# Scattered expert sums read back two jobs earlier and added in four jobs, in a fused decoder block

## Chip, core and metric

One NeuronCore of a Trainium2 chip runs the whole program; the other cores are idle. The metric is the device time of one execution in microseconds (us). PE is TensorE's matmuls, DVE is VectorE, ACT is ScalarE, POOL is GpSimd, SP is SyncE, which here only issues DMAs.

## What is computed

A decoder block on 512 tokens of 1024 features: one input projection, a sparse attention over the 128 keys that an indexer picks (DSA), a sliding-window attention with sinks (SWA), a gated merge, an output projection, a first layer norm, and a mixture of experts with a second layer norm. What the change touches is the mixture:

```python
combine = (jax.nn.one_hot(expert_id, N_EXPERTS) * top_w[..., None]).sum(1)   # two experts a token
for e in range(N_EXPERTS):                                                   # 32 experts
    h = jax.nn.silu(xt @ w_gate[e]) * (xt @ w_up[e])
    out = out + combine[:, e:e + 1] * (h @ w_down[e])
x = layer_norm(ALPHA * x + ffn, ln2_g, ln2_b)
```

## The kernel before

The kernel is one straight program written in a tile framework. A planner of that framework sets each engine's order by its own estimate of time, except for instructions that are pinned to the program's order; it also chooses which buffer of a pool a new tile gets, and puts in the waits. The attention stages fill about the first 330 us, the merge, the output projection, the first norm and the routing go to about 420 us, and the experts follow.

**Pages.** Nearly all large data live in one pool of PAGES (22) buffers of 1 MiB, 128 partitions by 2048 floats (`page`, L158 before the change). A page of weights, of accumulators, of gathered rows, of values read back: all come from there, and a DMA that loads a new page waits until the page's earlier use is over. Smaller tiles of 512 floats come from `temp`: four buffers with the tag "ms", five with the tag "pt".

**Experts.** Each expert is given 64 slots. The work is a list of 17 jobs, numbered here from 0 by their place in the loop at the end (`for n, w in enumerate(work)`): jobs 0 to 7 and 9 to 16 take two experts each, job 8 is one tile for tokens beyond an expert's 64 slots (the overflow job). A job of two experts needs six pages of weights, in this order: the first half of gate and up for both experts, the second half for both (the second pair), and down for both. `stage`, called three jobs ahead, issues them on SP's queue by `load_pieces` (L751, L754).

**A job.** PE multiplies the gathered rows with gate and up in 32 products of 0.22 us (`up_part`), ACT and DVE make the hidden values h (`hidden`, L1124 and L1126), PE turns the next job's rows and h, then multiplies h with the down weights (`down_half`). Then the sums leave in one of two ways:

- Jobs 0 to 7 (SCATTER): the scaled sums go by an indirect DMA of POOL to a DRAM tensor `yp`, which has two places a token (`scattered`).
- Jobs 8 to 16: `down_proj` splits the scaled sums into a high and a low half (yh, yl; yy for the overflow job), each in a tile of 512 floats, `places` makes a matrix of token places (ct), and `combine` adds them: PE multiplies place and halves into a bank named qt, and DVE adds the bank to the accumulator `acc` (L1227). These products are run in the next job, behind its gate and up products; in job 16, between them.

**Read back.** What lies in `yp` is read back after all scatters, two pages for blocks 0 and 1, two for blocks 2 and 3 (`back_load`, L1204, at the end of jobs 10 and 11), and DVE adds them to `acc` one job later (`back_add`, L1212, jobs 11 and 12, four adds of 128x1024 each).

**The end.** The second norm's weights g2 (named ln2, gain and offset of 0.5 MiB each, L1332 and L1333) are issued between the last job's up and down pages. In job 16 DVE and ACT centre the first block with the gain as soon as its sums are complete (`centre`, L110 by a helper), before the last hidden product; `rest` finishes the four blocks and the rows of the last job.

Of the kernel before, what the change touches and what calls it, by code (L numbers as in the profile page):

```python
# [20 lines left out]
P = 128  # L21
# [10 lines left out]
RMS_EPS = 1e-6  # L32
PAGES = 22
WARM = 14
# [14 lines left out]
DUMMY = 1  # L49
G2_AT = 4  # L50
BR_AT = (5, 7)
# [23 lines left out]
K_EARLY = 1  # L75
BACK_AT = 10
LAST_N = (0, 1, 1, 2, 1, 2, 1, 0)
# [53 lines left out]
def block_kernel(ctx: ExitStack, tc: tile.TileContext, xT, x, w_tm, w_in, w_uv, w_br, w_out, relb, oh,  # L131
# [31 lines left out]

    def temp(dt, name, tag="ms"):
        return pages.tile([P, 512], dt, name=name, tag=tag, bufs={"ms": 4, "pt": 5}[tag])

# [369 lines left out]
    def swa_out(b, Ls):  # L536
        n = P if b == 0 else 2 * P
        py = pv_bank()
        parts = [(s, g) for s in range(n // P) for g in range(2)]
        pts = {}  # L540

        def turn(s, g):
            tp = tr_bank()
            for i in range(4):
                nc.tensor.transpose(tp[:, i * P:(i + 1) * P], Ls[g * 4 + i][:, s * P:(s + 1) * P], ident)
            pt = temp(F32, "ptb", "pt")
            if g == 0:
                nc.scalar.activation(pt, tp, AF.Copy)
            else:
                nc.vector.tensor_copy(pt, tp)  # L550
            pts[s, g] = pt

        turn(*parts[0])
        for x in range(len(parts)):
            if x + 1 < len(parts):
                turn(*parts[x + 1])
            fill(SWA_FILL[1])
            s, g = parts[x]
            nc.tensor.matmul(py[g * 64:(g + 1) * 64], vb[:, b + 1 - n // P + s, g * 64:(g + 1) * 64], pts[s, g],  # L559
                             start=(s == 0), stop=(s == n // P - 1))  # L560
        pv = py.rearrange("p (i t) -> p i t", i=4)
        ts = slice(b * P, (b + 1) * P)
        nc.scalar.activation(ybh[:, :, ts], pv, AF.Copy)
        nc.vector.tensor_sub(ybl[:, :, ts], pv, ybh[:, :, ts].bitcast(F32))
# [11 lines left out]

    post["q"] = post_q
    lg = {0: swa_logits(0)}
    swa_probs(0, *lg[0])
# [50 lines left out]
    def dsa_out(h, Ls):  # L630
# [4 lines left out]
        def turn(g):  # L635
            tp = tr_bank()
            w = 0
            for s in g:
                for b in range(s, NB):
                    nc.tensor.transpose(tp[:, w:w + P], Ls[b][:, s * P:(s + 1) * P], ident)  # L640
                    w += P
            ph, pl = temp(F32R, "ptah", "pt"), temp(F32R, "ptal", "pt")
            nc.scalar.activation(ph[:, :w], tp[:, :w], AF.Copy)
            nc.vector.tensor_sub(pl[:, :w], tp[:, :w], ph[:, :w].bitcast(F32))
            pts[g] = (ph, pl)
# [54 lines left out]

    need("q0")
    lg = {0: dsa_logits(0)}
    for h in range(8):
# [457 lines left out]
    def down_proj(hT, dn, w_):  # L1161

        r = []
        if len(dn) == 2:
            for hf in range(2):
                py = down_half(hT, dn, hf)
                yh_, yl_ = temp(F32R, "yh", "pt"), temp(F32R, "yl", "pt")
                nc.scalar.activation(yh_, py, AF.Copy, scale=w_)
                nc.vector.scalar_tensor_tensor(yl_, py, w_, yh_.bitcast(F32), op0=ALU.mult, op1=ALU.subtract)
                r.append((yh_, yl_))  # L1170
            return r
# [6 lines left out]
        for s in range(2):  # L1178
            yy = temp(F32R, "yy", "pt")
            a, b = (slice(z * 64, (z + 1) * 64) for z in (s, 1 - s))  # L1180
# [26 lines left out]

    def back_add(q, r):
        for b in range(2):
            for t in r:  # L1210
                a = acc[2 * q + b]
                nc.vector.tensor_add(a, a, t[:, b * D:(b + 1) * D])  # L1212

    def places(tk_):
        ct = temp(F32R, "ct", "pt")
        nc.vector.tensor_scalar(ct, iot, tk_, None, op0=ALU.is_equal)
        return ct
# [104 lines left out]
    work.insert(OV_AT, "ov")  # L1322
    jobs = {}

    def stage(w):
        if w == "ov":
            jobs[w] = overflow_tile(0.0)
        else:
            pg = functools.partial(gather, idx[:, w:w + 1]) if w else None
            if w == 15:  # L1330
                load_pieces(6 * w + G2_AT)
                nc.sync.dma_start(g2[:, 0:D], bcast(ln2_g, D))  # L1332
                nc.sync.dma_start(g2[:, D:2 * D], bcast(ln2_b, D))  # L1333
            load_pieces(6 * w + 6)
            es = (w, w + 16)
# [103 lines left out]

    early, back, done_early = {}, {}, False  # L1440
    for n, w in enumerate(work):
        if n % 2 == 0 and 4 + n < 16:
            slots(4 + n, 6 + n)
        if n == 2:
            overflow_tiles()
        if n + 4 == len(work):
            g2 = page(F32, "ln2")
        if n + 3 < len(work):
            stage(work[n + 3])
        _, up, dn, tk_, w_ = jobs.pop(w)  # L1450
        last = n + 1 == len(work)
# [34 lines left out]
        if not last:  # L1486
# [4 lines left out]
            if w in SCATTER:  # L1491
                scattered(w, hT, dn, w_)
                late = []
            else:
                y = down_proj(hT, dn, w_)
                late = combine(places(tk_), y, then if n + 2 == len(work) else None)
        for q in range(2):
            if n == BACK_AT + q:
                back[q] = back_load(q)
            if n == BACK_AT + q + 1:  # L1500
                back_add(q, back.pop(q))
    pick(pz, [1], [0])
# [108 lines left out]
```

## Time and profile before

| | us |
|---|---|
| median of three runs | 714.94 (714.76 to 715.67) |
| the profiled execution, its own time | 714.15 |
| its span, on which the times of the rows are counted from 0 | 712.3 |
| PE busy | 650.9 (91%) |
| DVE busy | 394.5 (55%) |
| ACT busy | 261.3 (37%) |

The page divides the span in 40 slices of 17.8 us. A digit is the busy share of an engine in a slice in tenths. Each page of 1 MiB is one DMA, cut over 16 DMA engines. The views used below are the page, the list of who waited for whom, the order of time of one engine or queue, the instructions of one tile, groups of instructions, and busy times in chosen stretches.

### The profile page before, as it was taken

To read this page: it belongs to the slowest core of one execution; us is meant where nothing else is said; L and a number is where in the kernel's file an instruction comes from. 1 tells how busy PE (TensorE), PEld (TensorE's weight loads), DVE (VectorE), ACT (ScalarE), POOL (GpSimd) and SP (SyncE) were. 2 spreads that over 40 slices of the span, in tenths; PEclk is the share of its full clock that TensorE was granted. 3 is DMA by queue.
4 is the path that set the end of the run, shared out by engine and by line. 5 is a ranking of instruction groups with operands and counts; after the bars stand their busy time and mean duration, and the time that the engine had idled before them with its cause. 6 is when DMAs were issued, how large, how long until landed. Compare 5 with 4: busy or idle time off the path is not lost.

```text
span 712.3 us, 9305 instructions
## 1 busy us (share of the span) xinstructions
PE 650.9 (91%) x3394; PEld 435.8 (61%) x3394; DVE 394.5 (55%) x968; ACT 261.3 (37%) x552; POOL 90.9 (13%) x93
## 2 busy tenths in 40 slices
PE   7999998999999999999999989999998990679990
PEld 4788886766788878778899963334343440334430
DVE  6685999867444443667627882422135340654484
ACT  5563422867355445744214232121131120112260
POOL 0010000000000000012201333222221110110083
PEclk9999999999999999999999999999999996799996
DMA  8972511011411111154957779999999999998002
GB/s 326 359 253 73 193 60 59 2 60 59 178 60 59 60 60 59 61 178 163 385 220 296 265 268 375 421 418 419 416 418 420 418 417 418 414 420 361 15 19 120
DMA packets 34748, 164.65 MB, mean 231 GB/s; under 512 B 5977, under 2 KB 11361, under 8 KB 18828
## 3 DMA queue, kind: packets, MB, share of 16 engines
q1 hardware_dynamic: 26636, 147.98, 52.6%
q0 software_dynamic: 5968, 12.90, 5.1%
q10 hardware_dynamic: 2096, 3.15, 1.3%
q8 instruction: 28, 0.46, 0.3%
q14 instruction: 20, 0.16, 0.1%
HBM read 156.62 MB, written 16.29 MB: 243 GB/s over the span
## 4 chain that ended last, share of the span: by engine, by line
PE 65%; DMA 16%; DVE 14%; issue 2%; ACT 1%; POOL 1%; POOLq 0%; SPq 0%; DVEq 0%; ACTq 0%
PE mm L177 10%; PE mm L179 9%; PE mm L178 9%; DMA wexp<-in_w_up_dram 9%; PE mm L1076 8%; PE pv L1076 5%; PE qt L1076 4%; DMA wexp<-in_w_dn_dram 3%; DMA back<-yp 3%; DVE pgS L429 3%; DVE mx L427 2%; PE pv L559 2%; DVE whl L174 1%; PE tr L640 1%; DVE zb L110 1%
## 5 line engine op out<-in xcount | busy, mean ns | idle before, releaser
L177 PE MATMUL mm<-xh,whl 128*128 128x512 f32 (+1 forms) x272 | 108.4, 399 | 0.8 <-ACT xh L173 0.8
L178 PE MATMUL mm<-xl,whl 128*128 128x512 f32 (+1 forms) x272 | 106.3, 391 | 0.8 <-DVE xl L174 0.8
L179 PE MATMUL mm<-xh,whl 128*128 128x512 f32 (+1 forms) x272 | 106.2, 391 | 0.0
L1076 PE MATMUL mm<-wexp,xg 128*64 128x512 f32 x448 | 102.7, 595 | 1.8 <-DMA wexp<-in_w_up_dram 1.8
L1076 PEld LDWEIGHTS mm<-wexp,xg 128*64 128x64 f32 x448 | 31.7, 137 | 60.6 <-issue 55.6
L177 PEld LDWEIGHTS mm<-xh,whl 128*128 128x128 f32 x272 | 51.7, 190 | 12.7 <-issue 3.6
L179 PEld LDWEIGHTS mm<-xh,whl 128*128 128x128 f32 x272 | 51.5, 189 | 12.1 <-issue 2.5
L178 PEld LDWEIGHTS mm<-xl,whl 128*128 128x128 f32 x272 | 51.5, 189 | 10.0 <-DVE xl L174 1.1
L174 DVE TENSOR_TENSOR whl<-wraw,whl 128x1024 fp32r<-128x1024 f32 x34 | 41.5, 1221 | 25.7 <-ACT whl L173 24.0
L1076 PE MATMUL pv<-wexp,hT 128*64 128x512 f32 x240 | 55.3, 603 | 0.0
L796 POOL TENSOR_TENSOR tg<-tg 128x512 f32<-128x512 f32 x8 | 12.1, 1516 | 300.3 <-DVE tg L698 296.1
L1126 DVE TENSOR_TENSOR h<-h,mm 128x256 f32<-128x256 f32 x14 | 5.9, 420 | 66.0 <-ACT h L1124 66.0
L1076 PE MATMUL qt<-yh,ct 128*128 128x512 f32 x48 | 21.0, 437 | 22.8 <-DVE acc L1227 22.8
L173 ACT ACTIVATE whl<-wraw 128x1024 fp32r<-128x1024 f32 x34 | 35.7, 1054 | 14.1 <-DMA wraw<-in_w_in_dram 7.7
L1124 ACT ACTIVATE h<-mm 128x256 f32<-128x256 f32 x14 | 5.4, 384 | 94.4 <-PE mm L1076 94.4
L1227 DVE TENSOR_TENSOR acc<-acc,qt 128x512 f32<-128x512 f32 x56 | 34.3, 679 | 5.2 <-PE qt L1076 5.2
L1076 PEld LDWEIGHTS pv<-wexp,hT 128*64 128x64 f32 x240 | 16.8, 139 | 31.9 <-issue 27.4
L177 PE MATMUL mm<-woh,merged 128*128 128x256 f32 x120 | 36.3, 302 | 0.0
L1093 ACT ACTIVATE xg<-qt 128x512 f32<-128x512 f32 x32 | 18.0, 596 | 45.8 <-PE qt L1076 45.8
L178 PE MATMUL mm<-wol,merged 128*128 128x256 f32 x120 | 34.0, 283 | 0.0
L179 PE MATMUL mm<-woh,merged 128*128 128x256 f32 x120 | 33.9, 283 | 0.0
L1083 POOL MEMSET xg<- 128x1024 f32 x16 | 15.2, 953 | 137.0 <-PE qt L1076 137.0
(387 smaller groups left out, 1311.2 us busy)
## 6 DMA issues: line engine op xcount, KB each, us to landing
wexp<-in_w_up_dram SPq DMA_DIRECT2D x64, 1024.0 KB, 20.7
wexp<-in_w_dn_dram SPq DMA_DIRECT2D x31, 1024.0 KB, 20.8
wraw<-in_w_in_dram SPq DMA_DIRECT2D x16, 1024.0 KB, 4.9
yp<-routes SPq DMA_DIRECT2D x8, 512.0 KB, 8.5
braw<-in_w_br_dram SPq DMA_DIRECT2D x4, 1024.0 KB, 4.8
woraw<-in_w_out_dram SPq DMA_DIRECT2D x4, 1024.0 KB, 7.2
back<-yp SPq DMA_DIRECT2D x4, 1024.0 KB, 20.3
xraw<-in_xT_dram SPq DMA_DIRECT2D x4, 512.0 KB, 7.0
```

Source lines behind the costliest of these rows:

```text
L173: nc.scalar.activation(hi, raw, AF.Copy)
L174: nc.vector.tensor_sub(lo, raw, hi.bitcast(F32))
L177: nc.tensor.matmul(o, a[0], b[0], start=start, stop=False)
L178: nc.tensor.matmul(o, a[0], b[1], start=False, stop=False)
L179: nc.tensor.matmul(o, a[1], b[0], start=False, stop=stop)
L427: pin(nc.vector.max(out=mx, in_=acc))
L429: pin(nc.vector.match_replace(out=acc, in_to_replace=mx, in_values=acc, imm_value=GONE))
L559: nc.tensor.matmul(py[g * 64:(g + 1) * 64], vb[:, b + 1 - n // P + s, g * 64:(g + 1) * 64], pts[s, g], start=(s == 0), stop=(s == n // P - 1))
L1076: return lambda *a, **k: (pin if self.n else (lambda i: i))(getattr(nc.tensor, f)(*a, **k))
L1083: nc.gpsimd.memset(pg, 0.0)
L1093: nc.scalar.activation(c, banks[q], AF.Copy)
L1227: nc.vector.tensor_add(a, a, pc)
```

## The change

Five things are edited.

1. `BACK_AT` goes from 10 to 8: the back pages are issued at the end of jobs 8 and 9.
2. The adds are spread: in each of the jobs 11 to 14 one page, which is two adds of 128x1024.
3. PAGES goes from 22 to 23. The tag "pt" with its five tiles is gone; in its place a page of the pool holds four temporaries (`four_temps`, `temp4`), taken once for SWA, once for DSA, and once at job 8 for the halves of all following jobs. The tag "ms" has five buffers instead of four and now holds `ct` too.
4. The second norm's weights are issued after the last job's down pages.
5. The page for them is taken in `stage`, at the time of the load.

```diff
-PAGES = 22
+PAGES = 23
-G2_AT = 4
-BACK_AT = 10
+BACK_AT = 8
+BACK_ADD = 11
...
-    def temp(dt, name, tag="ms"):
-        return pages.tile([P, 512], dt, name=name, tag=tag, bufs={"ms": 4, "pt": 5}[tag])
+    def temp(dt, name):
+        return pages.tile([P, 512], dt, name=name, tag="ms", bufs=5)
+    turns = {"n": 0}
+    def four_temps(dt):
+        turns["page"] = page(dt, "four")
+    def temp4():
+        i = turns["n"] % 4
+        turns["n"] += 1
+        return turns["page"][:, i * 512:(i + 1) * 512]
...
-            pt = temp(F32, "ptb", "pt")
+            pt = temp4()
...
-            ph, pl = temp(F32R, "ptah", "pt"), temp(F32R, "ptal", "pt")
+            ph, pl = temp4(), temp4()
...
-                yh_, yl_ = temp(F32R, "yh", "pt"), temp(F32R, "yl", "pt")
+                yh_, yl_ = temp4(), temp4()
...
-            yy = temp(F32R, "yy", "pt")
+            yy = temp4()
...
-    def back_add(q, r):
+    def back_add(q, t):
         for b in range(2):
-            for t in r:
-                a = acc[2 * q + b]
-                nc.vector.tensor_add(a, a, t[:, b * D:(b + 1) * D])
+            a = acc[2 * q + b]
+            nc.vector.tensor_add(a, a, t[:, b * D:(b + 1) * D])
     def places(tk_):
-        ct = temp(F32R, "ct", "pt")
+        ct = temp(F32R, "ct")
...
+            load_pieces(6 * w + 6)
             if w == 15:
-                load_pieces(6 * w + G2_AT)
-                nc.sync.dma_start(g2[:, 0:D], bcast(ln2_g, D))
-                nc.sync.dma_start(g2[:, D:2 * D], bcast(ln2_b, D))
-            load_pieces(6 * w + 6)
+                norm2.append(page(F32, "ln2"))
+                nc.sync.dma_start(norm2[0][:, 0:D], bcast(ln2_g, D))
+                nc.sync.dma_start(norm2[0][:, D:2 * D], bcast(ln2_b, D))
...
+                if combined == 0:
+                    four_temps(F32R)
+                combined += 1
                 y = down_proj(hT, dn, w_)
...
-        for q in range(2):
-            if n == BACK_AT + q:
-                back[q] = back_load(q)
-            if n == BACK_AT + q + 1:
-                back_add(q, back.pop(q))
+        if 0 <= n - BACK_AT < 2:
+            back[n - BACK_AT] = back_load(n - BACK_AT)
+        if 0 <= n - BACK_ADD < 4:
+            back_add((n - BACK_ADD) // 2, back[(n - BACK_ADD) // 2].pop(0))
```

SP's queue before, from the last down page of job 13 to the first page of job 15. A row is a DMA: line, what is written, what is read. `wexp` is a page of weights, `back` a page read back, `yp` the scattered sums:

```order
L754 DMA wexp_4865<-in_w_dn_dram 128x2048
L1204 DMA back_4960<-yp_114 128x2x1024
L1204 DMA back_4962<-yp_114 128x2x1024
L751 DMA wexp_4964<-in_w_up_dram 128x2048
L751 DMA wexp_4966<-in_w_up_dram 128x2048
L751 DMA wexp_4968<-in_w_up_dram 128x2048
L751 DMA wexp_4970<-in_w_up_dram 128x2048
L754 DMA wexp_4972<-in_w_dn_dram 128x2048
L754 DMA wexp_4974<-in_w_dn_dram 128x2048
L1204 DMA back_5073<-yp_114 128x2x1024
L1204 DMA back_5075<-yp_114 128x2x1024
L751 DMA wexp_5077<-in_w_up_dram 128x2048
```

and of the change, from the last down page of job 11 to the first page of job 13:

```order
L767 DMA wexp_4623<-in_w_dn_dram 128x2048
L1217 DMA back_4678<-yp_114 128x2x1024
L1217 DMA back_4680<-yp_114 128x2x1024
L764 DMA wexp_4682<-in_w_up_dram 128x2048
L764 DMA wexp_4684<-in_w_up_dram 128x2048
L764 DMA wexp_4686<-in_w_up_dram 128x2048
L764 DMA wexp_4688<-in_w_up_dram 128x2048
L767 DMA wexp_4690<-in_w_dn_dram 128x2048
L767 DMA wexp_4692<-in_w_dn_dram 128x2048
L1217 DMA back_4772<-yp_114 128x2x1024
L1217 DMA back_4774<-yp_114 128x2x1024
L764 DMA wexp_4798<-in_w_up_dram 128x2048
```

Each pair of back pages stands two jobs, twelve pages of weights, further forward in the queue; the weights of jobs 12 and 13 stand behind them.

DVE before, from the halves of job 10 to the additions of job 12 (`yl` a low half, `ct` places, `h` hidden values, `acc<-acc,back` an add of a page read back, `acc<-acc,qt` one of PE's additions):

```order
L1169 SCALAR_TENSOR_TENSOR yl<-pv,wsl,yh 128x512 x2
L1216 TENSOR_SCALAR ct<-iot,tok 128x512
L1126 TENSOR_TENSOR h<-h,mm 128x256
L1212 TENSOR_TENSOR acc<-acc,back 128x1024 x4
L1227 TENSOR_TENSOR acc<-acc,qt 128x512 x8
L1169 SCALAR_TENSOR_TENSOR yl<-pv,wsl,yh 128x512 x2
L1216 TENSOR_SCALAR ct<-iot,tok 128x512
L1126 TENSOR_TENSOR h<-h,mm 128x256
L1227 TENSOR_TENSOR acc<-acc,qt 128x512 x4
L1212 TENSOR_TENSOR acc<-acc,back 128x1024 x4
L1227 TENSOR_TENSOR acc<-acc,qt 128x512 x4
```

and of the change, from the hidden values of job 11 to the second add of job 12:

```order
L1139 TENSOR_TENSOR h<-h,mm 128x256
L1239 TENSOR_TENSOR acc<-acc,qt 128x512 x8
L1228 TENSOR_SCALAR ct<-iot,tok 128x512
L1224 TENSOR_TENSOR acc<-acc,back 128x1024 x2
L1182 SCALAR_TENSOR_TENSOR four<-pv,wsl,four 128x512 x2
L1139 TENSOR_TENSOR h<-h,mm 128x256
L1239 TENSOR_TENSOR acc<-acc,qt 128x512 x8
L1228 TENSOR_SCALAR ct<-iot,tok 128x512
L1224 TENSOR_TENSOR acc<-acc,back 128x1024 x2
```

The adds came in two lots of four, ahead of or among PE's additions; they now come in four lots of two, behind a job's places and ahead of its own halves.

DVE before, around the halves of the overflow job (`yy`; `G` is a table that finds a job's slots):

```order
L1132 TENSOR_TENSOR h<-h,mm 64x256
L1182 SCALAR_TENSOR_TENSOR yy<-pv,ovs,yy 64x512
L1216 TENSOR_SCALAR ct<-iot,ovs 128x512
L1182 SCALAR_TENSOR_TENSOR yy<-pv,ovs,yy 64x512
L1227 TENSOR_TENSOR acc<-acc,qt 128x512
L1126 TENSOR_TENSOR h<-h,mm 128x256
L1227 TENSOR_TENSOR acc<-acc,qt 128x512 x7
L971 TENSOR_TENSOR G<-iot,routes 128x512 x2
```

and of the change:

```order
L1145 TENSOR_TENSOR h<-h,mm 64x256
L1228 TENSOR_SCALAR ct<-iot,ovs 128x512
L1139 TENSOR_TENSOR h<-h,mm 128x256
L1228 TENSOR_SCALAR ct<-iot,tok 128x512
L984 TENSOR_TENSOR G<-iot,routes 128x512 x2
L1195 SCALAR_TENSOR_TENSOR four<-pv,ovs,four 64x512 x2
L1239 TENSOR_TENSOR acc<-acc,qt 128x512 x8
```

The overflow job's two halves now stand behind the hidden values, the places and the slot tables of the next job.

## Rows read from the trace of the kernel before

**Rows 1.** The page's part 2: forty slices of the span.
```profile
PE   7999998999999999999999989999998990679990
...
PEclk9999999999999999999999999999999996799996
...
GB/s 326 359 253 73 193 60 59 2 60 59 178 60 59 60 60 59 61 178 163 385 220 296 265 268 375 421 418 419 416 418 420 418 417 418 414 420 361 15 19 120
```
**Rows 2.** Who waited for whom, PE, 440 to 712 us: us in total, times, longest.
```profile
PE qt L1076 <- DVE acc L1227: 27.2, 2, 22.8
```
**Rows 3.** PE in order of time: start us, us, line, op, [idle before].
```profile
579.51 7.04 PE L1076 MATMUL mm<-wexp,xg 128*64 128x512 f32 x32
...
611.60 0.80 PE L1076 MATMUL qt<-yh,ct 128*128 128x512 f32 x1 [22.79 <-DVE acc L1227]
...
619.38 7.04 PE L1076 MATMUL mm<-wexp,xg 128*64 128x512 f32 x32
...
634.90 1.83 PE L1076 MATMUL qt<-ident,xg 128*128 128x128 f32 x8 [4.38 <-DVE acc L1227]
...
641.04 7.03 PE L1076 MATMUL mm<-wexp,xg 128*64 128x512 f32 x32
...
672.33 1.89 PE L110 MATMUL mm<-wexp,xg 128*64 128x512 f32 x8
...
679.03 1.08 PE L110 MATMUL mm<-wexp,xg 128*64 128x512 f32 x4
```
**Rows 4.** DVE in order of time.
```profile
606.06 2.36 DVE L1212 TENSOR_TENSOR acc<-acc,back 128x1024 f32<-128x1024 f32 x2 [18.61 <-DMA back<-yp]
...
629.63 4.62 DVE L1212 TENSOR_TENSOR acc<-acc,back 128x1024 f32<-128x1024 f32 x4
...
685.55 2.12 DVE L110 SCALAR_TENSOR_TENSOR zb<-acc,mv,ln 128x768 f32<-128x768 f32 x1
```
**Rows 5.** Stretches: us, busy (x) of PE, PEld, DVE, ACT, POOL, granted clock, DMA.
```profile
611.00:614.60 3.60, 3.00 (x7) 2.42 (x8) 3.56 (x7) 0.00 (x0) 0.00 (x0) 0.50 1.02 422
635.00:638.50 3.50, 3.50 (x14) 1.92 (x16) 1.64 (x3) 1.20 (x2) 1.44 (x2) 0.51 1.00 417
```
**Rows 6.** SP's queue in order of time, jobs 12 to 16 and back pages.
```profile
553.96 7.80 SPq L751 DMA_DIRECT2D wexp<-in_w_up_dram  x4
...
569.73 7.85 SPq L751 DMA_DIRECT2D wexp<-in_w_up_dram  x4
...
586.03 2.85 SPq L1204 DMA_DIRECT2D back<-yp  x2
590.99 7.81 SPq L751 DMA_DIRECT2D wexp<-in_w_up_dram  x4
...
611.05 9.33 SPq L751 DMA_DIRECT2D wexp<-in_w_up_dram  x4
...
626.76 7.85 SPq L751 DMA_DIRECT2D wexp<-in_w_up_dram  x4
```
**Rows 7.** The tile wexp, 560 to 662 us: issues (ns), and us to landing.
```profile
L751 SPq DMA_DIRECT2D wexp<-in_w_up_dram x17: 327/328/572, 561.4 to 634.3; - x17
...
DMA to landing us min/median/max: 17.9/20.9/22.0
```
**Rows 8.** The tile back, whole span.
```profile
DMA to landing us min/median/max: 19.9/20.3/20.7
```
**Rows 9.** Who waited for whom, SP's queue, 400 to 660 us.
```profile
SPq L751 <- PE pv L1076: 25.0, 5, 16.3
```
**Rows 10.** Groups of DVE, 530 to 560 us: busy us, mean ns, idle before.
```profile
L1182 DVE SCALAR_TENSOR_TENSOR yy<-pv,ovs,yy 64x512 fp32r<-64x512 f32 x2 | 1.5, 749 | 5.7 <-ACT yy L1181 5.7
...
L971 DVE TENSOR_TENSOR G<-iot,routes 128x512 bf16<-128x512 f32 x2 | 1.3, 682 | 0.0
```
**Rows 11.** Stretches of the attention stage, columns as in rows 5.
```profile
110.00:140.00 30.00, 26.88 (x131) 20.05 (x130) 27.91 (x88) 17.18 (x55) 0.00 (x0) 1.00 0.10 36
140.00:200.00 60.00, 60.00 (x275) 41.28 (x275) 36.71 (x100) 35.33 (x87) 0.00 (x0) 1.00 0.24 88
```

More of the change, by code (lines that the diff above doesn't have):

```diff
@@ L577, in block_kernel @@
     post["q"] = post_q
+    four_temps(F32)
     lg = {0: swa_logits(0)}
@@ L1322, in block_kernel @@
     work.insert(OV_AT, "ov")
-    jobs = {}
+    jobs, norm2 = {}, []
     def stage(w):
@@ L1438, in rest @@
                                      in_=zs[:, 0:D], in_offset=None, bounds_check=T - 1, oob_is_err=False)
-    early, back, done_early = {}, {}, False
+    early, back, done_early, combined = {}, {}, False, 0
     for n, w in enumerate(work):
@@ L1445, in block_kernel @@
             overflow_tiles()
-        if n + 4 == len(work):
-            g2 = page(F32, "ln2")
         if n + 3 < len(work):
             stage(work[n + 3])
+        if n + 4 == len(work):
+            g2 = norm2[0]
         _, up, dn, tk_, w_ = jobs.pop(w)
@@ L1494, in block_kernel @@
             else:
+                if combined == 0:
+                    four_temps(F32R)
+                combined += 1
                 y = down_proj(hT, dn, w_)
                 late = combine(places(tk_), y, then if n + 2 == len(work) else None)
-        for q in range(2):
-            if n == BACK_AT + q:
-                back[q] = back_load(q)
-            if n == BACK_AT + q + 1:
-                back_add(q, back.pop(q))
+        if 0 <= n - BACK_AT < 2:
+            back[n - BACK_AT] = back_load(n - BACK_AT)
+        if 0 <= n - BACK_ADD < 4:
+            back_add((n - BACK_ADD) // 2, back[(n - BACK_ADD) // 2].pop(0))
     pick(pz, [1], [0])
```

## The prediction

> **What bounds the kernel now.** I read the page's busy lines first, then the waits of PE, then the order of time on PE, DVE and SP's queue. The first view shows that the second half of the span is not like the first: from the 26th slice to the 36th the DMA engines move about 418 GB/s without a break, and PE, at 9 tenths or more nearly everywhere, falls to 0 and 6 tenths in two slices, where its granted clock falls too [rows 1]. So two resources must be watched together: the stream of expert weights, and PE, which eats it.
>
> The list of waits names what stops PE there: 27.2 us in two waits, both on DVE's add into acc [rows 2]. In order of time, PE's first products of jobs 12, 13, 14 and 16 begin at 579.51, 619.38, 641.04 and 672.33 [rows 3]. Jobs 14 and 15 are undisturbed and take 31.29 us, 15.65 each; the steps 12 to 13 and 13 to 14 take 39.87 and 21.66. The excess is 24.2 + 6.0 = **30.2 us**. DVE's rows say why: its eight adds of the pages read back stand in two lumps, the first waits 18.61 us for its page to land, and the adds of PE's results into acc, which free the banks that PE wants, queue behind [rows 4]. The excess is more than the 27.2 us of waits because PE comes back from each at a granted clock of 0.5, the lower of its two levels (1.2 GHz) [rows 5].
>
> **What this buys at most.** SP's queue issues the pages of weights in order, one every 2.5 us, and a page lands about 20.9 us (back pages and those beside them 20.3) after its issue [rows 6 to 8]. Adding that to the issue of the fourth page of a job (the end of its row, less the 0.33 us of one issue) gives when its up projection has all it needs: job 12 at 582.3, job 13 at 598.2, job 14 at 618.8, job 15 at 640.4, job 16 at 655.2. PE wants the second pair 3.5 us after a job begins (half of a row of 7.04 us [rows 3]), so job 12 wants it at 583.0 and has it 0.7 us before. PE and the stream were level when the stall came. The stall let the stream run ahead, and without it PE must wait for weights. Not all of the 30.2 us can be had.
>
> **The change, part by part.**
>
> *Read back earlier.* The four back pages go two jobs forward in SP's queue, before the weights of jobs 12 and 13. One pair takes 590.99 - 586.03 = 4.96 us of the queue [rows 6]. So the weights of job 12 come 5.0 us later than now, those of job 13 9.9, those of job 14 5.0, those of jobs 15 and 16 as now. The stream moves the same bytes. Walk PE through it, with 8.6 us from the end of one job's products to the start of the next (15.65 less 7.04):
>
> - job 12 starts at 579.5, wants its second pair at 583.0, has it at 587.3, ends its products at 590.8;
> - job 13 starts at 599.4, wants it at 602.9, has it at 608.1, ends at 611.6;
> - job 14 starts at 620.2, wants it at 623.7, has it at 623.8, ends at 627.3;
> - job 15 starts at 635.9, wants it at 639.4, has it at 640.4, ends at 643.9;
> - job 16 starts at 652.5; its products stand among the previous job's additions, so the second pair is wanted 6.7 us after the start (672.33 to 679.03 [rows 3]), at 659.2, and is there at 655.2.
>
> Job 16 started at 672.33; the gain is **19.8 us**. About 10 of the 30 us come back as waits for weights.
>
> The Trainium skill, on its page "DMA: Bandwidth & Descriptors", section "Where 436 GB/s comes from", says that between HBM and SBUF the HBM side binds at some 358 GB/s. By that figure a page would take 2.93 us, the two pairs 11.7 instead of 9.9, and the gain would be 1.8 us less. The trace disagrees: 418 GB/s over eleven slices [rows 1], so the sum keeps 2.5 us a page.
>
> *Two blocks in each of jobs 11 to 14.* The eight adds, 2.36 us a pair [rows 4], are the same work; now two stand behind the job's places and ahead of its halves on DVE. The first back page takes the place in the queue that the first weight of job 12 has now, an issue at 553.96, so it lands at about 574.9 and its two adds are done at 577.3; the halves behind them come from PE's down products of job 11, which are the last thing before job 12's start at 579.5. Cost 0: what little a half is late lies under the 7 us of job 12's up products, and only after these does PE want it. Without that cover, 2.4 us a job on DVE, 9.4 in all.
>
> *A page for four temporaries.* The pool has one page more, and the four temporaries take it from job 8 on, and in the two attention stages. Until job 8 the weights have one page more to run ahead, and before that SP had waited up to 16.3 us at a time for PE to free a page [rows 9]. A page is worth 2.5 us of the stream, if it is issued into time that DMA has free; at worst nothing. I take 1.5, nearer the upper end because the wait for a page is long. Carried through the walk above (every landing 1.5 us earlier), job 16 starts at 651.0: a gain of **21.3 us**.
>
> *The order of the overflow job's halves.* On DVE they now stand behind the next job's hidden product, its places and two slot tables: two tables 1.3 us and two halves 1.5 [rows 10]. PE's additions of the overflow job wait for them: 0 to 2.8 us, at job 9. I take 2.8, but it costs nothing at the end: PE then comes to job 12 at 582.3, wants the second pair at 585.8, and that lands at 585.8; job 13 waits for its weights in any case.
>
> *The attention stage.* Four slots replace five, and the scheduler sets some of PE's products there in another order. From 140 us on PE is full in it (60.00 of 60 us), and the 30 us before lack 3.1 [rows 11]; the same products remain, so a new order gains at most those 3.1 and loses, by the same row, as much again: -3 to +3 us. I take 0; the 1.5 us above has room for it.
>
> *Second norm's weights last.* The last two pages of weights come 2.5 us earlier, where nothing waits for them. The norm's own land behind them, at 655.2 + 4 x 2.5 - 1.5, some 663 at the latest for both halves and 1.3 earlier for the half that DVE wants first. DVE wants it at 685.55 now [rows 4], so at 664.2 after. Hidden, with 1 to 2.5 us of cover. If it is late, job 16's hidden product stands behind that row on DVE, and PE's last products behind the hidden product: microsecond for microsecond.
>
> **Sum.** The profiled execution took 714.15 us, the median of the runs is 714.94, 0.8 above. 714.94 - 21.3 = **693.6**; I say 693.5.
>
> **The rivals.**
>
> *Less waiting for weights* (0.13). If the stream gains the whole page and the pairs wait less, the bound is the last page: job 16's second pair at 655.2 - 2.5, so a start at 646.0 and a gain of 26.3: 688.6. For: 30.2 us are there. Against: SP's steady 2.5 us.
>
> *The clock* (0.17). Today a wait of 4.38 us is followed by a stretch of 3.5 us at clock 0.51 [rows 3, 5]. The new waits at jobs 12 and 13 are of that size (4.3 and 5.2), and may each bring such a stretch, in which 1.75 us are lost, part of it under the wait for the second pair. One to two stretches: 695 to 697. The Trainium skill, "TensorE: Matmul & The Clock Gate", section "HAM oscillation — how this bites in real kernels", tells of a kernel that waited for DMA at every piece of work and came back slow every time; by that rule each new wait pays, and the time is the upper end of this rival. The trace agrees for both waits on acc: each is followed by the slow clock [rows 5].
>
> *The norm's weights or the attention order cost what I called hidden* (0.15): 2 to 4 us, 695.5 to 698.
>
> *Starved of pages: slower* (0.03). The back pages are now held for three to five jobs. With 23 pages, 2 of acc, 2 of gathered rows, 1 of temporaries and 4 read back leave 14; a running job holds 6; 8 are in flight (20.9 over 2.5). That is just enough. If the pool's assignment makes a job's first weight wait for the job directly before it, a job takes 20.9 + 7.0 = 27.9 us instead of 15.65, in jobs 11 to 14 +49; less the 30.2 removed, 734. It decides from two pages more held than I count. Against: from 400 to 660 us SP waited for PE only five times, 25.0 us in all, 16.3 of them at once [rows 9].
>
> *It doesn't do what it says* (0.02): the reads still land late for the adds. SP's new order speaks against it.
>
> **How the numbers follow.** The forecast (691 to 695) has 0.50. Below 688.5 and above 699 I leave some 2 in 10: the range is 688.5 to 699.0, from the first rival's bound to no page gained with two slow stretches. A measurement of this kernel tells 0.2% (1.4 us) from no change. Faster 0.95, the same 0.02, slower 0.03.
>
> **What would show it.** Right: PE has no wait on acc's add left; instead one on weights at jobs 12 and 13, 3 to 6 us each; DVE's adds of back pages stand in four pairs with no idle time before them; DMA stays near 418 GB/s till some 660; job 16's first product at about 651. Wrong: SP waiting for PE between 550 and 640, DVE waiting for the norm's weights, or a job 16 that starts before 646 or after 656.

## The result, and the profile after

The changed kernel takes **697.32 us** (median of four runs, 697.11 to 699.07), against 715.31 us for the kernel before. The ratio is 0.9746, with a 95% interval of 0.9714 to 0.9777: faster by 2.5%. The forecast was 693.5 us in a range of 688.5 to 699.0. The sign and the mechanism came out; the time is 3.8 us longer than forecast, and the experiments are mostly about those 3.8 us. The profiled execution took 697.48 us, its span is 695.7, so the span is 16.6 us shorter than before.

The page's part 2 of the changed kernel answers to [rows 1]:

```profile
PE   7899998999999999999999987999999799899990
...
PEclk9999999999999999999999999899999899989995
...
GB/s 315 377 247 82 212 62 60 1 61 61 182 60 62 61 60 8 83 154 125 338 326 195 317 243 381 258 418 419 419 417 417 421 415 415 417 419 419 371 35 132
```

The hole of PE is gone: no slice but the last is under 7 tenths. The stream of weights keeps its 418 GB/s from the 27th slice on. The 26th slice (435 to 452 us) is new in another way: DMA moves only 258 GB/s there.

Who PE waited for, 330 to 712 us, largest first, answers to [rows 2]:

```profile
PE qt L1089 <- DMA xg<-x1d,idx: 4.7, 1, 4.7
PE mm L1089 <- DMA wexp<-in_w_up_dram: 3.1, 2, 1.7
PE qt L1089 <- DVE four L1195: 2.6, 2, 1.9
```

The 27.2 us of waits for DVE's add into acc are gone. The waits for weights that the forecast put in their place are there, but smaller and both at job 13 (3.1 us in all, not some 10 over jobs 12 and 13), and the largest wait is one that nobody forecast: for gathered rows (xg), before the first expert.

PE in order of time, the first products of jobs 0, 12, 13 (in two pieces), 14 and 16, and the waits, answers to [rows 3]:

```profile
433.52 1.97 PE L1089 MATMUL qt<-ident,xg 128*128 128x128 f32 x8 [4.75 <-DMA xg<-x1d,idx]
...
435.85 1.98 PE L1089 MATMUL mm<-wexp,xg 128*64 128x512 f32 x4
...
587.44 7.04 PE L1089 MATMUL mm<-wexp,xg 128*64 128x512 f32 x32
...
604.65 1.04 PE L1089 MATMUL mm<-wexp,xg 128*64 128x512 f32 x2 [1.37 <-DMA wexp<-in_w_up_dram]
607.38 10.01 PE L1089 MATMUL mm<-wexp,xg 128*64 128x512 f32 x30 [1.69 <-DMA wexp<-in_w_up_dram]
...
625.98 7.04 PE L1089 MATMUL mm<-wexp,xg 128*64 128x512 f32 x32
...
657.27 1.89 PE L110 MATMUL mm<-wexp,xg 128*64 128x512 f32 x8
```

Job 16 begins at 657.27, 15.1 us earlier than before; the forecast said 651.0. Job 12 begins 7.9 us *later* than before. From job 16 on the kernel takes 38.4 us instead of 40.0, so the 16.6 us are 15.1 and 1.5.

DVE's adds of the pages read back, three of the four pairs, answer to [rows 4]:

```profile
585.24 2.34 DVE L1224 TENSOR_TENSOR acc<-acc,back 128x1024 f32<-128x1024 f32 x2
...
600.90 2.34 DVE L1224 TENSOR_TENSOR acc<-acc,back 128x1024 f32<-128x1024 f32 x2
...
623.78 2.34 DVE L1224 TENSOR_TENSOR acc<-acc,back 128x1024 f32<-128x1024 f32 x2
```

No add waits: the bracket that said 18.61 is gone. The pairs run straight behind the places, as the new order has it.

**Where the unforecast wait comes from.** The last quarter of the rows x1d is written to DRAM by POOL's queue, and the gathers read it. POOL's queue and SP's queue of the changed kernel, around that write:

```profile
417.06 0.58 POOL L916 DMA_DIRECT2D x1d<-acc  x1 [1.72 <-DVE routes L931]
...
424.84 1.32 POOL L1097 DMA_INDIRECT xg<-x1d,idx  x1 [4.81 <-DVE info L954]
```

```profile
416.58 11.71 SPq L764 DMA_DIRECT2D wexp<-in_w_up_dram  x4
428.80 13.57 SPq L767 DMA_DIRECT2D wexp<-in_w_dn_dram  x2
```

and the same two queues of the kernel before:

```profile
416.20 0.58 POOL L903 DMA_DIRECT2D x1d<-acc  x1 [1.73 <-DVE routes L918]
...
422.12 1.10 POOL L1084 DMA_INDIRECT xg<-x1d,idx  x1 [2.96 <-DVE info L933]
```

```profile
423.65 6.70 SPq L751 DMA_DIRECT2D wexp<-in_w_up_dram  x4
```

Before, SP had no free page and issued the next weights at 423.65. With one page more it issues them at 416.58, half a microsecond ahead of the write of x1d. The write then takes 6.9 us from issue to landing (3.0 before), the gather behind it is issued 2.7 us later, and it takes 8.6 us (4.5 before) beside two more pages of weights, which SP issued at 423.00 and 423.42, ahead of it. The trace puts POOL's wait down to DVE's row `info`, but the gather reads DVE's `idx`, which was done at 421.0, and x1d, whose write landed at 423.9 (417.06 + 6.9); the gather is issued 0.9 us after that. PE's first expert begins 4.5 us later than before, and job 1, behind the low clock, 6.2 us later (449.37 against 443.19).

Stretches of the changed kernel (columns as in [rows 5]), behind the wait for rows, and at job 13. The last column is GB/s; from 434 to 442 us the kernel before had moved 349:

```profile
434.00:442.00 8.00, 8.00 (x31) 3.51 (x32) 0.00 (x0) 2.15 (x4) 1.95 (x2) 0.67 0.46 176
...
607.30:617.40 10.10, 10.02 (x31) 2.89 (x31) 0.00 (x0) 0.00 (x0) 0.00 (x0) 0.70 1.02 419
```

After each of the two waits PE runs at a granted clock of about two thirds on average, between its two levels of 1.2 and 2.4 GHz.

### The profile page after: what moved, and what is told of

Its sections match the earlier page's. It is cut to its first block, busy times and chain, and to the rows that moved or that the text cites. A ratio compares the mean times of both kernels' runs of the same rounds, so it can differ in the third digit from the quotient of the medians.

```text
span 695.7 us, 9272 instructions
## 1 busy us (share of the span) xinstructions
PE 652.4 (94%) x3394; PEld 435.3 (63%) x3394; DVE 394.5 (57%) x968; ACT 260.7 (37%) x552; POOL 94.9 (14%) x93
## 4 chain that ended last, share of the span: by engine, by line
PE 75%; DVE 13%; DMA 7%; issue 1%; ACT 1%; POOL 1%; SPq 0%; POOLq 0%; DVEq 0%; ACTq 0%
PE mm L1089 15%; PE mm L188 9%; PE mm L189 9%; PE mm L190 9%; PE pv L1089 7%; PE qt L1089 6%; DMA wexp<-in_w_up_dram 3%; DVE pgS L440 3%; DVE mx L438 2%; PE pv L570 2%; DMA wraw<-in_w_in_dram 2%; DVE whl L185 1%; PE tr L652 1%; DMA xg<-x1d,idx 1%; DVE zb L110 1%
## 5 line engine op out<-in xcount | busy, mean ns | idle before, releaser
L1089 PE MATMUL mm<-wexp,xg 128*64 128x512 f32 x448 | 105.4, 614 | 3.1 <-DMA wexp<-in_w_up_dram 3.1
L184 ACT ACTIVATE whl<-wraw 128x1024 fp32r<-128x1024 f32 x34 | 35.7, 1053 | 16.5 <-DMA wraw<-in_w_in_dram 12.9
L1089 PEld LDWEIGHTS pv<-wexp,hT 128*64 128x64 f32 x240 | 16.9, 139 | 32.3 <-issue 27.9
L622 DVE CUSTOM_DVE_ANT_0 La<-qk,bias 128x128 f32<-128x128 f32 (+3 forms) x32 | 15.3, 489 | 30.8 <-PE qk L621 28.2
L1089 PE MATMUL qt<-four,ct 128*128 128x512 f32 x104 | 29.6, 429 | 2.6 <-DVE four L1195 2.6
```

Source lines behind the costliest of these rows:

```text
L184: nc.scalar.activation(hi, raw, AF.Copy)
L622: nc.vector.tensor_tensor_reduce(Ls[b], o, ta_bias[h][:, T - n:], 1.0, -3.0e38, ALU.add, ALU.max, m4[:, b:b + 1])
L1089: return lambda *a, **k: (pin if self.n else (lambda i: i))(getattr(nc.tensor, f)(*a, **k))
```

## The experiments

**Theory A:** the new page is not a gain but the loss. It lets SP put weights ahead of the write of x1d; PE begins the experts late and at the low clock; pages come free only as PE uses them, so the stream of weights falls behind too. **Theory B:** the late start costs nothing, since the stream decides at job 13 anyway, and the page helps the stream. **Rival C:** the gain doesn't come from the read-back at all. Each ratio is to runs of the kernel before that were made beside it (medians 715.31 to 716.71), with a 95% interval; the starts are those of the first products in the profiled execution.

| run | median us | ratio | span | job 0 | job 12 | job 16 |
|---|---|---|---|---|---|---|
| before | 715.31 | 1 | 712.3 | 431.33 | 579.51 | 672.33 |
| the change | 697.32 | 0.9746 (0.9714 to 0.9777) | 695.7 | 435.85 | 587.44 | 657.27 |
| backonly | 695.57 | 0.9723 (0.9699 to 0.9747) | 693.8 | 431.68 | 580.92 | 653.83 |
| hold | 693.37 | 0.9688 (0.9673 to 0.9703) | 692.5 | 430.64 | 579.79 | 652.72 |
| x1dsp | 693.47 | 0.9686 (0.9669 to 0.9704) | 694.0 | 433.83 | 584.26 | 654.60 |
| late | 717.83 | 1.003 (1.0015 to 1.0045) | 714.8 | 433.99 | 584.89 | 674.89 |
| hold9 | 690.04 | 0.9640 (0.9619 to 0.9661) | 687.9 | 429.39 | 577.73 | 649.05 |
| hold8 | 692.63 | 0.9663 (0.9641 to 0.9685) | 691.2 | 429.84 | 577.79 | 651.72 |
| holdg2 | 691.98 | 0.9664 (0.9642 to 0.9685) | 690.5 | 428.97 | 578.03 | 650.92 |
| holdno | 682.09 | 0.9525 (0.9506 to 0.9545) | 680.3 | 428.70 | 576.93 | 640.62 |
| hold10 | 690.34 | 0.9640 (0.9622 to 0.9658) | 689.3 | 429.93 | 578.48 | 647.25 |
| before9 | 692.97 | 0.9678 (0.9661 to 0.9694) | 692.5 | 431.17 | 581.35 | 652.05 |
| spread9x | 691.89 | 0.9658 (0.9633 to 0.9683) | 690.1 | 433.19 | 584.95 | 651.54 |

**late: the read-back as before, all else changed.**

```diff
-BACK_AT = 8
+BACK_AT = 10
...
+        for q in range(2):
+            if n == BACK_AT + q:
+                back[q] = back_load(q)
+            if n == BACK_AT + q + 1:
+                for t in back.pop(q):
+                    back_add(q, t)
```

> The changed kernel with the read-back as it was before: back pages issued at jobs 10 and 11, four adds each in jobs 11 and 12; pages, temporaries and the norm's place stay changed. Theories A and B: PE's waits on DVE's add into acc come back, 20 us or more in all, and the time is 712 to 722. Rival C (the gain came from the pages or from the order, not from the read-back): no such wait, below 705.

The gain is gone, and 0.3% more. Who PE waited for, 440 to 715 us:

```profile
PE mm L1089 <- DVE h L1139: 19.5, 2, 18.5
PE qt L1089 <- DVE acc L1239: 4.8, 1, 4.8
```

The larger wait shows on another row, the hidden values, which stand on DVE behind the four adds; both together are 24.3 us, against 27.2 before. Rival C falls: the whole gain is the read-back's, and with the old read-back the other parts together cost 0.3%.

**backonly: the kernel before with the read-back edit alone.** Its diff to the kernel before is `BACK_AT`, `BACK_ADD`, `back_add` and the last four lines of the change; on PE, ACT and POOL no instruction moves.

> The kernel before with the read-back edit alone: back pages issued at jobs 8 and 9, two adds in each of jobs 11 to 14; 22 pages, the five pt tiles and the norm's place as before. Theory A (the new page is what cost: it let SP put a page of weights ahead of the last write of x1d, job 1's rows came 6.8 us later, PE began the experts 6 us later, and the stream of weights fell behind with it): job 0's products begin at 431 to 432, job 12's at about 579.5, job 13's second pair lands near 608 (612.5 in the changed kernel), and the time is 692 to 696, below the changed kernel's 697.3. Theory B (the stream alone sets job 13, and the page gives it 2.5 us): the time is 697 to 701, above the changed kernel.

It gave 695.57 us: in the range of A, below that of B. Its interval still overlaps the changed kernel's, so the time alone does not part them; the starts do. Job 0 begins at 431.68, job 12 at 580.92, and job 16 3.4 us ahead of the changed kernel. The read-back alone gives all of the gain.

**hold: the page of temporaries is never given back.** The halves of jobs 8 to 16 use the page that DSA took, so that SP finds no extra page from 416 us on.

```diff
-                if combined == 0:
-                    four_temps(F32R)
-                combined += 1
```

> The changed kernel, but the halves of jobs 8 to 16 reuse the page of temporaries that DSA took, so that page is not free for weights between the attention and job 8. Theory A: the last write of x1d lands by about 420 and job 1's rows by 427 (423.8 and 433.4 in the changed kernel), PE has no wait for rows, job 0's products begin at 431 to 433, time 692 to 696. Theory B: job 0 begins earlier, but the time stays at 697 to 700, because job 13 waits for its weights either way.

It gave 693.37 us, with an interval that lies below the changed kernel's. PE in order of time, jobs 0, 12 and 13, and 16:

```profile
430.64 1.08 PE L1089 MATMUL mm<-wexp,xg 128*64 128x512 f32 x4
...
579.79 1.04 PE L1089 MATMUL mm<-wexp,xg 128*64 128x512 f32 x2 [0.58 <-DMA wexp<-in_w_up_dram]
582.19 4.75 PE L1089 MATMUL mm<-wexp,xg 128*64 128x512 f32 x16 [1.36 <-DMA wexp<-in_w_up_dram]
588.46 3.65 PE L1089 MATMUL mm<-wexp,xg 128*64 128x512 f32 x14 [1.52 <-DMA wexp<-in_w_up_dram]
...
601.12 1.04 PE L1089 MATMUL mm<-wexp,xg 128*64 128x512 f32 x2 [0.25 <-DMA wexp<-in_w_up_dram]
603.52 4.28 PE L1089 MATMUL mm<-wexp,xg 128*64 128x512 f32 x16 [1.37 <-DMA wexp<-in_w_up_dram]
609.19 3.65 PE L1089 MATMUL mm<-wexp,xg 128*64 128x512 f32 x14 [1.38 <-DMA wexp<-in_w_up_dram]
...
652.72 1.89 PE L110 MATMUL mm<-wexp,xg 128*64 128x512 f32 x8
```

The wait for rows is gone, and jobs 12 and 13 wait 3.5 and 3.0 us for weights. The stretch from 434 to 442 us of this kernel, against 176 GB/s and clock 0.67 of the changed one:

```profile
434.00:442.00 8.00, 8.00 (x42) 3.01 (x38) 1.10 (x3) 0.71 (x3) 1.03 (x1) 1.00 1.00 402
```

and SP's queue at job 13's weights, first of this kernel, then of the changed one:

```profile
579.72 9.09 SPq L764 DMA_DIRECT2D wexp<-in_w_up_dram  x4
```

```profile
583.26 7.80 SPq L764 DMA_DIRECT2D wexp<-in_w_up_dram  x4
```

So the page that was to bring the weights 1.5 us earlier brought them 3.5 us later than hold does. The lag is there long before job 13: SP's queue lags hold's by 3.5 us already at the overflow job's pages (499.29 against 495.82), and still at the first page of job 15 (615.21 against 611.70). Both links of theory A are seen; B, by which the late start costs nothing, falls.

hold is not the page alone, though. With it the planner's order around the overflow job is that of the kernel before again, so PE's wait of 2.65 us for the overflow job's halves is gone too. x1dsp, next, keeps that wait.

**x1dsp: the page stays, the write goes first.**

```diff
-        nc.gpsimd.dma_start(x1d[b * P:(b + 1) * P], z)
+        (nc.sync if b == NB - 1 else nc.gpsimd).dma_start(x1d[b * P:(b + 1) * P], z)
```

> The changed kernel with the last write of x1d issued on SP's queue, ahead of the page of weights that had overtaken it; the new page stays. Theory A: the write lands by about 420, job 1's rows by 428, PE's wait of 4.75 us is gone and with it the half clock behind it, job 0's products begin at 431 to 433, and the stream keeps the page it gained: 689 to 694. Theory B: 696 to 698.

It gave 693.47 us. The write lands 4.2 us after its issue, job 1's rows at 428.8 (424.37 + 4.4), and the wait for rows is gone. So the wait came from the order of the two DMAs, not from the number of pages as such. Yet the kernel is no better than hold, and job 0 begins only at 433.83, later than the expected 431 to 433. The edit has a side effect: POOL, which no longer issues the write, clears the pages for gathered rows 3.3 us sooner than in hold (415.36 against 418.71), now beside three DVE rows of the routing. POOL, then DVE:

```profile
415.36 1.86 POOL L1096 MEMSET xg<- 128x1024 f32 x2
```

```profile
415.18 2.08 DVE L110 TENSOR_SCALAR sel<-s 128x32 bf16<-128x32 f32 x1
415.27 1.99 DVE L110 SCALAR_TENSOR_TENSOR acc<-acc,rs,ln 128x512 f32<-128x512 f32 x1
415.94 1.33 DVE L110 COPY tops<-mx 128x1 f32<-128x1 f32 x1
```

In hold, without POOL beside them, the three take 0.18, 0.74 and 0.14 us. PE now waits 3.55 us for `tops` (its wait at this place is 1.6 to 1.9 us in the kernels with the write on POOL), and the 26 products behind that wait take 4.66 us instead of hold's 3.27, part of them at a granted clock of 0.50. So x1dsp shows where the wait for rows came from, but not what the page is worth with nothing else changed.

The first page of job 15 is issued at 611.70 in hold, 612.82 in backonly, 613.60 in x1dsp and 615.21 in the changed kernel: 1.1, 1.9 and 3.5 us behind hold. Job 16 begins 1.1, 1.9 and 4.6 us behind hold's. In the first two the stream alone accounts for the start; the changed kernel has 1.0 us more, at job 13 (below).

**holdno: what the read-back still costs.** hold without the four reads and their adds; jobs 0 to 7 are missing from the sums.

> The kernel 'hold' with the reads back and their adds left out, so jobs 0 to 7 are missing from the sums. This prices the read-back as it now stands. By the walk all waits for weights at jobs 12 and 13 go, PE runs 15.65 us a job, job 16 begins at 642 to 645, and the time is 682 to 686. If the four pages were hidden in the changed kernel: 691 to 693.

It gave 682.09 us; the list of waits has none for weights at jobs 12 to 16. The read-back costs 11.3 us in hold (693.37 - 682.09). About 10 us had been forecast as coming back in waits.

**hold9 and hold8: one page at a time.** `back_load` loads one page, and the places move:

```diff
-BACK_AT = 8
-BACK_ADD = 11
+BACK_AT = 9
+BACK_ADD = 12
...
-        if 0 <= n - BACK_AT < 2:
+        if 0 <= n - BACK_AT < 4:
```

(hold8 keeps 8 and 11.)

> The kernel 'hold' with the four back pages issued one in each of jobs 9 to 12 and added in jobs 12 to 15, instead of two in each of jobs 8 and 9 and adds in jobs 11 to 14. If the forecast's walk is right that PE waits at jobs 12 and 13 for as many pages as stand ahead of their weights, job 12 has no wait, job 13 waits for one page (about 2.5 us) instead of four, jobs 14 and 15 wait some 2 us each, job 16 begins at about 649 (652.7 in hold), and the time is 688 to 691. If the waits are set by the sum of bytes and not by the order, the time is that of hold, 692 to 694.

> The kernel 'hold' with the back pages issued one in each of jobs 8 to 11; the adds stay in jobs 11 to 14. By the walk job 12 waits 2.1 us, job 13 some 2.9, job 14 some 2, job 15 some 2.6, job 16 begins at about 651.3, 1.4 us ahead of hold: 690.5 to 693. If the order doesn't matter: 692 to 694, no different from hold.

hold9 gave 690.04 us with job 16 at 649.05, both as the walk had them; the waits, below, came out somewhat shorter than the 2.5, 2 and 2 us expected. From job 0 to job 16 it takes 219.66 us, hold 222.08; so 2.4 of the 3.3 us between their medians can be seen in the experts, in single profiles. PE at jobs 13, 14 and 15:

```profile
600.52 3.65 PE L1089 MATMUL mm<-wexp,xg 128*64 128x512 f32 x14 [2.01 <-DMA wexp<-in_w_up_dram]
...
619.00 3.65 PE L1089 MATMUL mm<-wexp,xg 128*64 128x512 f32 x14 [1.80 <-DMA wexp<-in_w_up_dram]
...
636.82 3.65 PE L1089 MATMUL mm<-wexp,xg 128*64 128x512 f32 x14 [1.13 <-DMA wexp<-in_w_up_dram]
```

hold8 gave 692.63 us, within its range, but its interval overlaps hold's. Of jobs 12 to 16 only 12 and 14 wait, 2.6 us each; hold8 has them 18 products into the job, and pays for each a second time at the low clock:

```profile
585.01 5.34 PE L1089 MATMUL mm<-wexp,xg 128*64 128x512 f32 x14 [2.60 <-DMA wexp<-in_w_up_dram]
...
622.00 5.34 PE L1089 MATMUL mm<-wexp,xg 128*64 128x512 f32 x14 [2.62 <-DMA wexp<-in_w_up_dram]
```

The same 14 products take 3.65 us in hold9. That is 1.7 us lost behind each wait, in which the stream caught up, so jobs 13 and 15 did not wait, where some 2.9 and 2.6 us had been expected.

**holdg2: the norm's weights where they were.** `load_pieces(6 * w + 4)` stands ahead of the norm's two DMAs again, the rest of the pieces behind.

> The kernel 'hold' with the second norm's weights issued between the last job's up and down pages, as in the kernel before. The forecast priced this part of the change at nothing: the time is that of hold within 1 us (692.4 to 694.4). Rival: the norm's weights were just in time in the changed kernel or the down pages are now late: 1 to 3 us either way, with a wait of DVE for ln or of PE for the down weights.

It gave 691.98 us, 0.4 below the expected range. From job 10's first product to job 16's it takes 105.17 us (545.75 to 650.92), hold 105.04 (547.68 to 652.72); the rest lies ahead of job 10, where the two programs are the same. Neither DVE nor PE waits for the norm or the down weights. On each engine the two programs run the same instructions in the same order. This part of the change is worth nothing measurable.

**hold10, before9 and spread9x: what is left.** hold10 puts the pages of hold9 one job later, the last two together in job 12. before9 is the kernel before with hold9's read-back alone. spread9x is x1dsp with it.

> The kernel 'hold9' with the back pages one place later still: one in each of jobs 10 and 11, two in job 12, added in jobs 13, 14 and 15. If the waits follow the pages ahead of each job's weights, job 13 has no wait (2.01 us in hold9), jobs 14 and 15 wait as before, and job 16, whose second pair stands behind the same bytes, begins 0 to 2 us earlier: 688 to 690. Rival: the last pages land too late for the adds of job 15, and DVE keeps PE waiting there: 691 to 694.

> The kernel before with the read-back of 'hold9' alone: one back page in each of jobs 9 to 12, added in jobs 12 to 15; 22 pages, the five pt tiles and the norm's place as before. If the pages and temporaries add nothing (theory A and the price of hold against backonly), the time is that of hold9, 688 to 692. If they do: 693 or more.

> The changed kernel, which keeps its new page free for weights until job 8, with both repairs: the last write of x1d ahead of the weights on SP's queue, and the back pages one in each of jobs 9 to 12 with adds in jobs 12 to 15. If the new page is worth the 1.5 to 2.5 us that the forecast gave it once the write is out of its way: 687 to 689, below hold9 (690.0). If it is worth nothing: 689.5 to 692.

hold10 gave 690.34 us, 0.3 above its first range. Job 13 no longer waits and job 16 begins 1.8 us earlier, but then waits 1.6 us for its own weights, and its last stage is 3.2 us longer than hold9's (42.05 against 38.85): 2.2 of it up to the centring of the first block, where the wait for its own weights falls, 0.3 from there to DVE's last row, and 0.8 between that row and the last write to the result. The bytes ahead of job 16 are the same. The last adds did not keep PE waiting.

before9 gave 692.97 us, at the edge of the second expectation. From job 9 to job 16 it takes 123.66 us (528.39 to 652.05), hold9 123.69 (525.36 to 649.05), so the difference of 3 us lies ahead of job 9. The three profiled kernels with five pt tiles (before, backonly, before9) begin job 0 at 431.2 to 431.7, the six with hold's page at 428.7 to 430.6. Counted from the last product of the input projection, which ends anywhere from 291.2 to 293.6 us in these runs, the six begin job 0 after 137.4 to 137.5 us, before and before9 after 140.3, backonly after 138.8. Of before's 2.9 us, 1.5 are the granted clock in the routing: 26 products behind a wait of 1.85 us took 4.73 us there, and 3.27 behind 1.65 us in hold. backonly, with the same wait of 1.85, took 3.27 too. Of the rest, 0.8 lies ahead of that wait's end and 0.6 behind these products; why stays open.

spread9x gave 691.89 us, in the range for a page that is worth nothing. But it has x1dsp's side effect (PE waits 3.55 us for `tops`, and job 0 begins 3.8 us behind hold9's), and its job 16 is only 2.5 us behind hold9's. What the free page is worth without that late start, no run shows. There is a hint that it is worth something: job 16 of spread9x has caught up 1.3 of those 3.8 us, and against hold x1dsp has caught up 1.3 of 3.2 and the changed kernel's stream 1.7 of 5.2, while backonly, without the free page, has caught up none of its 1.0. That is near the 1.5 us that the forecast gave the page, but it is read from single profiles and other things differ too. hold9 and hold10 have the lowest ratio of the complete kernels, 0.9640 against the change's 0.9746, with intervals apart from the change's; those of holdg2, hold8 and spread9x overlap theirs.

## Why the prediction was right in its sign and 3.8 us short

- **The bound, and what the waits would turn into: right.** No wait on acc's add is left; waits for weights took its place, in the changed kernel at job 13 alone (3.1 us), in hold at jobs 12 and 13. In hold, which is the walk without the page's 1.5 us, the walk's starts can be read against the trace: job 12 at 579.5 forecast and 579.79 measured, job 13 at 599.4 and 601.12, job 14 at 620.2 and 621.42, job 15 at 635.9 and 637.06, job 16 at 652.5 and 652.72. Its gain was 19.8 us, and the span of hold is 712.3 - 692.5 = 19.8 us shorter. A part of that agreement is luck: hold's experts begin 0.7 us earlier than before's; its waits come in three pieces a job, 3.5 and 3.0 us in all, where the walk had one of 4.3 and one of 5.2; and by medians hold gains 22.8 us (716.20 to 693.37).
- **A page for four temporaries: the step that failed.** "I take 1.5, nearer the upper end because the wait for a page is long." The text had priced the page "at worst nothing", on the ground that it could only let the stream run ahead, and had not asked what the earlier DMA would be issued ahead of. It collided with the write and the gathers on which PE waited. Job 16 came 6.3 us later than forecast (657.27 against 651.0), and so outside the 646 to 656 beyond which the prediction called itself wrong. At job 13 the products ended at 617.4, where the walk with the page had them end at 610.1 (608.1 - 1.5 + 3.5). Of these 7.3 us some 6 are the late stream: job 13's fourth page, issued at 590.7, landed 21.9 us later, at 612.6, where the walk had it at 606.6. The remaining 1.2 or so are the low clock. The 30 products took 10.01 us instead of 6.6 (at 0.22 each), but most of that lay under the wait for the fourth page: the 14 products behind it began at 613.80. One microsecond came back when job 15 did not have to wait. Whether the page itself is worth the 1.5 us stays open; what failed is that its cost was put at nothing.

```profile
L764 SPq DMA_DIRECT2D wexp<-in_w_up_dram x1: 328/328/328, 590.7 to 590.7; - x1
...
DMA to landing us min/median/max: 21.9/21.9/21.9
```

```profile
613.80 3.60 PE L1089 MATMUL mm<-wexp,xg 128*64 128x512 f32 x14
```

- **The other two differences go the other way.** The stage from job 16 on took 1.5 us less than before, which nothing in the forecast said; and the profiled execution now lies 0.2 above the median, where it lay 0.8 below. 6.3 - 1.5 - 1.0 = 3.8.
- **Two blocks in each job, cost 0: right.** The adds ran without a wait, and the back pages landed 21.3 to 22.1 us after issue (20.3 had been used).
- **The overflow job's halves: right in size.** PE waits 2.65 us for them and 0.5 more for the hidden values at job 9; 0 to 2.8 had been given. That it costs nothing at the end could not be read from the changed kernel, which was late anyway. x1dsp has the same order and a wait of 2.9 us; its job 16 is 1.9 us behind hold's, no more than its weights are, so there the wait was covered.
- **The attention stage, 0 within -3 to +3: nothing here contradicts it.** No run changed that stage alone; the kernels with hold's page begin job 0 1.4 to 2.9 us sooner behind the projection than those with five pt tiles, and up to 1.5 of that is the clock in the routing.
- **The norm's weights, hidden: right** (holdg2).
- **The clock rival (0.17, one to two stretches, 695 to 697): it came, for another reason.** There was a slow stretch at job 13, and one at job 0 where no wait had been foreseen. The Trainium skill's page "TensorE: Matmul & The Clock Gate", section "HAM oscillation — how this bites in real kernels", would have each new wait pay. The trace agrees for the changed kernel and for hold8, and not for hold or hold9, whose waits of up to 2.01 us left the clock at 1.00.
- **SP waiting for PE between 550 and 640 us, named as a sign of a wrong forecast, hardly occurred**: 2.4 us in eight waits. The prediction's row of 25.0 us in five waits [rows 9] is one line and one releaser of that view; in all SP waited for PE some 66 us in 29 waits from 400 to 660 us in the kernel before, so that reason against the rival of too few pages was weaker than it looked. In the changed kernel it waited for PE where nobody had looked, 12.9 us at once from 429 us, for want of a page that late PE still held.

## What to carry to other kernels

A buffer more is not "at worst nothing". Before pricing it, find the first DMA that it will let go earlier, and list what is issued on every queue in the next few microseconds: if one of those transfers is on the critical path, the free buffer puts a rival ahead of it. When a stream and an engine are level, place a necessary extra transfer in pieces, so that no job's data stand behind more than one new piece at a time; hold9 is 3.3 us below hold, 2.4 of them in the experts. Where the pieces go matters: one job earlier (hold8) the gain is not clear of noise, one job later (hold10) it is no larger.

## What the runs showed of the hardware that was not expected

**Waits of like size, and a clock that fell behind some of them.** Waits of 0.25, 1.37 and 1.38 us with products between them (hold, job 13) left the granted clock at 1.00, and so did a single one of 2.01 us (hold9). A single one of 2.60 us (hold8), and 1.37 and 1.69 us with only two products between them (the change), were followed by averages of 0.68 and 0.70. The length of a wait alone does not decide it: the routing's wait of 1.85 us was followed by clock 0.50 in the kernel before and by full clock in backonly, which is the same program up to there.

```profile
585.00:590.30 5.30, 5.29 (x15) 1.46 (x15) 0.00 (x0) 0.00 (x0) 0.00 (x0) 0.68 1.01 418
```

```profile
600.50:604.10 3.60, 3.58 (x15) 1.06 (x15) 0.00 (x0) 0.00 (x0) 0.00 (x0) 1.00 1.03 424
```

The first row is hold8's stretch behind its wait, the second hold9's.

**Two engines beside each other.** The length of one DVE row in the last stage goes with when POOL began the row beside it. Changed kernel, DVE and then POOL (before: 2.12 us from 685.55 [rows 4], POOL from 685.56):

```profile
670.01 1.01 DVE L110 SCALAR_TENSOR_TENSOR zb<-acc,mv,ln 128x768 f32<-128x768 f32 x1
```

```profile
670.10 4.00 POOL L110 TENSOR_TENSOR ahl<-acc,ahl 128x512 fp32r<-128x512 f32 x2 [0.37 <-ACT ahl L110]
```

With a lead of 0.09 us DVE took 1.01 us, with 0.01 us 2.12; POOL's two rows took 4.00 and 3.24. All thirteen kernels fall in with that: leads of 0.08 to 0.10 us go with 1.01, leads of 0.01 to 0.04 (before, holdno, late, hold10) with 2.12 to 2.15. It costs little at the end, because the rows behind it make up for it: from the start of this row to the end of DVE's last row it is 16.9 us in the kernel before and 16.7 in the changed one. So the 1.5 us that the last stage became shorter are 0.5 ahead of this row, 0.2 on DVE and 0.8 behind it, where the last write to the result waits for the writes ahead of it (it starts 1.8 us after DVE's last row before, 1.0 in the changed kernel):

```profile
704.28 1.04 POOL L110 DMA_INDIRECT out_dram<-zs,idx  x1 [4.41 <-DMA out_dram<-zb]
```

```profile
687.67 1.04 POOL L110 DMA_INDIRECT out_dram<-zs,idx  x1 [3.57 <-DMA out_dram<-zb]
```

Why these writes landed sooner is not shown. hold, with the short row, has a last stage of 39.8 us.

**A DMA delayed by one issued just ahead of it on another queue.** The write of 512 KB took 6.9 us instead of 3.0 when a page of 1 MiB had been issued 0.5 us before it from SP; in x1dsp, with the write ahead of the page, it took 4.2. The Trainium skill's page "DMA: Bandwidth & Descriptors", section "Queues, rings and completion order", says that each DMA engine takes turns, packet by packet, between the queues that have work for it. By that rule the write would share the engines with the page and not stand behind it. The trace does not decide it: the page, issued at 416.58, landed 6.1 us later, at 422.7, and the write 1.3 us after it.
